# Ranking the weight splits higher and moving a scan's stores to another queue in a hybrid layer's step

## The chip, the cores and the metric

The kernel runs on one core of one Trainium2 chip. The metric is the device time of that core in microseconds (us), the median of three executions. All arithmetic is in fp32; a matmul operand in fp32r is a rounded copy of an fp32 tile.

Engines are named as the profile names them: PE (TensorE, matmuls), DVE (VectorE), ACT (ScalarE), POOL (GpSimd) and SP (SyncE). SP does nothing here but issue DMA transfers. POOL issues transfers too, and does some elementwise work. Each engine carries out its own instructions strictly in their order, and waits at the head of that order for whatever the instruction needs.

## The reference, cut to what matters

One step of a decoder layer for 256 prompt tokens and 8 sample sequences of 4 tokens (288 columns in all), with an SSD branch, a GLA branch, cross attention into 256 memory rows, and a convolutional FFN:

```python
xn = _rmsnorm(x, p['norm_mix'])
z, xbc, dt_raw, q, k, v, r, g_lr, gate_a, gate_b = _split(xn @ p['w_in'], IN_SIZES)
...
y_ssd, ssd_state_new = _ssd_scan(...)          # 4 groups, state (heads, 64, 128) per sequence
branch_a = u @ p['w_ssd_out']
...
o, gla_state_new = _gla_scan(qh, kh, vh, glog, gla_state.astype(f32))   # 4 heads, state 256x512
branch_b = o @ p['w_gla_out']
merged = jax.nn.sigmoid(gate_a) * branch_a + jax.nn.sigmoid(gate_b) * branch_b
h = x + merged @ p['w_mix_out']
h = h + _cross_attend(_rmsnorm(h, p['norm_cross']), mem_k, mem_v, p['w_cq'], p['w_co'])
up = _rmsnorm(h, p['norm_ffn']) @ p['w_up']
...
h = h + (jax.nn.silu(gt) * a) @ p['w_down']
```

The updated states of both scans are outputs: for each GLA head one 256x512 state of the prompt and eight of the samples, 512 KB each.

## The kernel before

**Products.** Activations lie transposed in SBUF, features on the partitions, 288 columns of tokens. A weight tile of 512 KB (`raw`, three buffers) is loaded in SP's queue (`wload`, L108). Each of its halves, 128x512, is split by `wsplit`: ACT copies it to a rounded `whi` (L101), DVE subtracts to get the rest, `wlo` (L103); each has five buffers (`WB`). PE then makes three products per tile, `whi` by the high part of the activations (L133), `whi` by their low part (L134) and `wlo` by the high part (L137). One split feeds 12 matmuls of 128x288. The memory projections do the same with 128x512 matmuls (L315, L316, L319).

**Stages in order of time.** Memory keys and values (to about 207 us), the four SSD groups (to 665), the four GLA heads (to 1165), gates and the mix, cross attention (1432 to 1643), the FFN, and a short tail. Within a stage `weave` (L158) runs a stream of weight products and, between its steps, steps of a background generator such as a scan, so that the PE has products to do while the scan's small operations run elsewhere.

**What sets the order.** The framework orders each engine's instructions by a priority (at first the place in the program) and its own estimate of when operands are ready. Only the first memory projection is ordered by hand (`manual_schedule`, L344 on). The state loads are put under `keep_in_program_order`.

**The start.** `mem_load` brings 256 KB of memory rows, `wload` 512 KB of weights, in turns. PE first does 9 products of ones (L349), then transposes (L287), then the first products with weights (L315).

**An SSD group's norm.** DVE adds three squares (L898), PE sums them over the partitions (L909), ACT makes the reciprocal root (L205, L206, with a table load before each), DVE scales (L914) and splits (L171).

**A GLA head's scan** (`gla_scan`, L1000 to L1140). The prompt's state `sn` is made in two chunks (L1087 is the second chunk's update) and stored (L1099). Then `load_state` (L1008) brings the sample states `sin` of sequences 0 to 3. PE adds eight products of these to `la` (L1110, each shown as a weight load and two records), four updates follow (L1119 on PE, L1120 on DVE), and after each update the state is stored (L1123) and the state four further on is loaded. The second half does the same with sequences 4 to 7. The products of a half take the last loaded state first (`for j in (3, 2, 1, 0)`). `sn` and `sin` share six buffers.

**The other stores that the change touches.** `acum_d` (L498), the convolution's last rows (L592), an SSD group's prompt state (L753) and sample states (L872), and the merged gate pieces `ma` (L1165), all in SP's queue, between the weight loads.

## Time and profile before

| | us |
|---|---|
| median of 3 executions | 2574.29 |
| lowest and highest | 2574.22, 2579.31 |
| the profiled execution | 2576.44 |
| its span | 2574.7 |
| its mean granted PE clock | 0.997 |

The span is the time between the first and the last instruction of the profiled execution; its own time is 1.7 us longer. "Idle before, releaser" in a row is how long the engine stood still before that instruction, and what it had waited for. A matmul's record lasts longer than its share of the engine, since they overlap: what counts is the distance between two starts. The granted clock is a share of full speed. A row of the view of waits gives the waiting instruction, who ended the wait, and in total, how often, and the longest. Times of DMA "to landing" run from the issue of a transfer to its arrival.

### The profile page before, as it was taken

Reading aid. Unit: us, or ns where it says so; the run is one execution under the profiler, and the core shown is the slowest. Engines: PE = TensorE matmul, PEld = TensorE weight load, DVE = VectorE, ACT = ScalarE, POOL = GpSimd, SP = SyncE. Lnnn points to the kernel's source line nnn. Section 1 sums busy time; section 2 is a strip of 40 time slices with the busy share of each in tenths; the row PEclk is TensorE's granted clock in tenths of the full one; section 3 lists DMA queues with packets and bytes.
Section 4 is the critical chain, followed back from the end, with each engine's and each line's share of the span. In section 5 each row is a group of like instructions: output and inputs, shape, how many; then the busy total and the mean of one; then the engine's idle time right before and its main releaser. Section 6 shows DMA issues by size and latency. Waiting matters only on the chain. (4 is left out here: it accounts for less than half of the span.)

```text
span 2574.7 us, 50424 instructions
## 1 busy us (share of the span) xinstructions
PE 2554.8 (99%) x19119; PEld 2458.4 (95%) x19119; DVE 1714.8 (67%) x3623; ACT 1378.2 (54%) x2751; POOL 355.5 (14%) x519
## 2 busy tenths in 40 slices
PE   9999999999999999999999999999999999999998
PEld 7889999999999999999999989999999999999998
DVE  5656767687767666767566555567777677675765
ACT  7656547665463555544455544445545455454545
POOL 3002101110000000010000222202212122130200
PEclk9999999999999999999999999999999999999999
DMA  8766666666558575777666778755555555555553
GB/s 258 221 215 202 183 188 203 187 203 200 176 181 275 182 251 176 235 227 251 186 208 211 253 257 303 223 162 165 166 174 171 168 164 175 169 168 173 170 170 127
DMA packets 435203, 513.53 MB, mean 199 GB/s; under 512 B 23216, under 2 KB 385072, under 8 KB 434896
## 3 DMA queue, kind: packets, MB, share of 16 engines
q1 hardware_dynamic: 407568, 422.34, 53.5%
q0 software_dynamic: 27360, 87.96, 10.3%
q8 instruction: 150, 2.46, 0.4%
q14 instruction: 93, 0.76, 0.1%
q10 hardware_dynamic: 32, 0.01, 0.0%
HBM read 464.74 MB, written 45.48 MB: 198 GB/s over the span
## 5 line engine op out<-in xcount | busy, mean ns | idle before, releaser
L103 DVE TENSOR_TENSOR wlo<-raw,whi 128x512 fp32r<-128x512 f32 x1464 | 991.5, 687 | 676.6 <-ACT whi L101 657.8
L101 ACT CAST whi<-raw 128x512 fp32r<-128x512 f32 x1464 | 897.2, 618 | 1000.0 <-PE acc L134 783.2
L133 PE MATMUL acc<-xn,whi 128*128 128x288 f32 (+1 forms) x1936 | 554.9, 302 | 0.0
L134 PE MATMUL acc<-xn,whi 128*128 128x288 f32 (+1 forms) x1936 | 541.5, 295 | 0.0
L137 PE MATMUL acc<-xn,wlo 128*128 128x288 f32 (+1 forms) x1936 | 412.1, 294 | 3.4 <-DVE wlo L103 3.4
L134 PE MATMUL acc<-hf,whi 128*128 128x288 f32 x1408 | 392.7, 295 | 0.0
L133 PE MATMUL acc<-hf,whi 128*128 128x288 f32 x1408 | 389.4, 292 | 0.0
L133 PEld LDWEIGHTS acc<-xn,whi 128*128 128x128 f32 (+1 forms) x1936 | 364.3, 188 | 9.3 <-issue 7.9
L134 PEld LDWEIGHTS acc<-xn,whi 128*128 128x128 f32 (+1 forms) x1936 | 364.6, 188 | 6.4 <-issue 4.1
L137 PEld LDWEIGHTS acc<-xn,wlo 128*128 128x128 f32 (+1 forms) x1936 | 311.1, 188 | 4.1 <-DVE wlo L103 4.1
L137 PE MATMUL acc<-hf,wlo 128*128 128x288 f32 x1408 | 296.2, 291 | 0.0
L134 PEld LDWEIGHTS acc<-hf,whi 128*128 128x128 f32 x1408 | 264.5, 188 | 0.1
L133 PEld LDWEIGHTS acc<-hf,whi 128*128 128x128 f32 x1408 | 264.1, 188 | 0.1
L137 PEld LDWEIGHTS acc<-hf,wlo 128*128 128x128 f32 x1408 | 225.9, 188 | 0.0
L1520 POOL COPY fsp<-fst 128x16 f32<-128x16 f32 x88 | 127.6, 1452 | 640.3 <-ACT fca L1526 286.5
L134 PE MATMUL acc<-pr,whi 128*128 128x288 f32 x704 | 196.5, 295 | 0.0
L133 PE MATMUL acc<-pr,whi 128*128 128x288 f32 x704 | 195.6, 294 | 0.0
L137 PE MATMUL acc<-pr,wlo 128*128 128x288 f32 x704 | 147.8, 291 | 0.0
L133 PE MATMUL acc<-un,whi 128*128 128x288 f32 x512 | 146.1, 301 | 0.0
L134 PE MATMUL acc<-un,whi 128*128 128x288 f32 x512 | 143.1, 295 | 0.5 <-DVE un L171 0.5
L134 PEld LDWEIGHTS acc<-pr,whi 128*128 128x128 f32 x704 | 132.3, 188 | 0.0
L133 PEld LDWEIGHTS acc<-pr,whi 128*128 128x128 f32 x704 | 132.1, 188 | 0.0
(515 smaller groups left out, 4243.1 us busy)
## 6 DMA issues: line engine op xcount, KB each, us to landing
raw<-in_w_in_dram SPq DMA_DIRECT2D x240, 512.0 KB
raw<-in_w_up_dram SPq DMA_DIRECT2D x176, 512.0 KB
raw<-in_w_down_dram SPq DMA_DIRECT2D x88, 512.0 KB
raw<-in_w_ck_dram SPq DMA_DIRECT2D x32, 512.0 KB
raw<-in_w_cv_dram SPq DMA_DIRECT2D x32, 512.0 KB
raw<-in_w_ssd_out_dram SPq DMA_DIRECT2D x32, 512.0 KB
sin<-in_state_gla_dram POOLq DMA_DIRECT2D x32, 512.0 KB, 6.2
out_dram<-sin SPq DMA_DIRECT2D x32, 512.0 KB
```

Of the source, the lines that this page charges most:

```text
L101: S.copy(hi, raw)
L103: V.tensor_tensor(lo, raw, hi, ALU.subtract)
L133: MM(a, hi[:, k, cs], xh, start=(k0 + s0 + k == 0), stop=False)
L134: MM(a, hi[:, k, cs], xl, start=False, stop=False)
L137: MM(a, lo[:, k, cs], xh, start=False, stop=(k0 + s0 + k == nk - 1))
L1520: G.tensor_copy(sp[:, :, 0:2], st.rearrange("p (b k) -> p b k", k=2))
```

## The change

- `wsplit` runs under `tc.high_priority(100)`: the splits of weights rank a hundred instructions higher in the order of ACT and DVE.
- 92 stores move from SP's queue to POOL's: the convolution's rows, the states of both scans, `acum_d` and `ma`.
- The first weight tile comes in two loads of 256 KB.
- Six products of ones stand on PE after the second transposes and before the first products with weights.
- x is loaded in every second step of the background, which has 28 steps instead of 24, and the squares of x are taken in another order. The masks' POOL operations stand later in the program.

```diff
+AHEAD = 100
...
     def wsplit(raw):
-        hi = wp.tile(list(raw.shape), F32R, tag="whi", bufs=WB, name="whi")
-        S.copy(hi, raw)
-        lo = wp.tile(list(raw.shape), F32R, tag="wlo", bufs=WB, name="wlo")
-        V.tensor_tensor(lo, raw, hi, ALU.subtract)
+        with tc.high_priority(AHEAD):
+            hi = wp.tile(list(raw.shape), F32R, tag="whi", bufs=WB, name="whi")
+            S.copy(hi, raw)
+            lo = wp.tile(list(raw.shape), F32R, tag="wlo", bufs=WB, name="wlo")
+            V.tensor_tensor(lo, raw, hi, ALU.subtract)
         return hi, lo
-    def wload(src):
+    def wload(src, apart=False):
         raw = wp.tile([P, src.shape[1], src.shape[2]], F32, tag="raw", bufs=RB, name="raw")
-        nc.sync.dma_start(out=raw, in_=src)
+        if apart:
+            for k in range(src.shape[1]):
+                nc.sync.dma_start(out=raw[:, k, :], in_=src[:, k, :])
+        else:
+            nc.sync.dma_start(out=raw, in_=src)
         return raw
...
             mem_prep(kk)
+            if kk == 1:
+                for _ in range(6):
+                    MM(wm[:, 0:P], ones, ones, start=True, stop=True)
...
         def x_norm():
...
-            xl = x_load()
-            for _ in range(4):
-                next(xl)
+            for step in range(23):
+                if step % 2 and step < 18:
+                    x_load(step // 2)
...
-        weave(chain(mem_proj(I["w_cv"], 0, o_pmv), mem_proj(I["w_ck"], 1, o_pmk)), x_norm(), 2 * KT, 24)
+        weave(chain(mem_proj(I["w_cv"], 0, o_pmv), mem_proj(I["w_ck"], 1, o_pmk)), x_norm(), 2 * KT, 28)
...
-            nc.sync.dma_start(out=acum_d, in_=acumT)
+            G.dma_start(out=acum_d, in_=acumT)
...
-                nc.sync.dma_start(out=o[:, c0:c0 + n * P].rearrange("k (t p) -> k t p", p=P), in_=st[r0:r1])
+                G.dma_start(out=o[:, c0:c0 + n * P].rearrange("k (t p) -> k t p", p=P), in_=st[r0:r1])
...
-        nc.sync.dma_start(out=o_pssd[0, h0:h0 + 8].rearrange("(t e) x n -> (e x) t n", e=2),
+        G.dma_start(out=o_pssd[0, h0:h0 + 8].rearrange("(t e) x n -> (e x) t n", e=2),
...
-                nc.sync.dma_start(out=o_sssd[2 * q + e, h0:h0 + 8].rearrange("(t e) x n -> (e x) t n", e=2),
+                G.dma_start(out=o_sssd[2 * q + e, h0:h0 + 8].rearrange("(t e) x n -> (e x) t n", e=2),
...
-        nc.sync.dma_start(out=o_pgla[0, h].rearrange("(k p) v -> p k v", p=P), in_=sprev)
+        G.dma_start(out=o_pgla[0, h].rearrange("(k p) v -> p k v", p=P), in_=sprev)
         for b in range(4):
             load_state(b)
...
-                nc.sync.dma_start(out=o_sgla[b, h].rearrange("(k p) v -> p k v", p=P), in_=sin)
+                G.dma_start(out=o_sgla[b, h].rearrange("(k p) v -> p k v", p=P), in_=sin)
                 if b + 4 < NB:
                     load_state(b + 4)
...
-            nc.sync.dma_start(out=(mg_d if t < 2 * GH else ma_d)[:, t - 3:t + 1, :], in_=ma[:, t - 3:t + 1, :])
+            G.dma_start(out=(mg_d if t < 2 * GH else ma_d)[:, t - 3:t + 1, :], in_=ma[:, t - 3:t + 1, :])
```

The changed kernel's numbers of lines differ by a few: L101 and L103 become L103 and L105, L133, L134 and L137 become L139, L140 and L143, L914 becomes L922, L1008 becomes L1016, L1099 becomes L1107, L1110 becomes L1118, L1123 becomes L1131.

POOL's order from the end of the SSD groups into the GLA heads, before (a row is a run of equal instructions, `x6` is six of them; `gw` is a gate's weights, `gq` a gate's piece):

```order
136 L699 DMA sin<-in_state_ssd_dram 128x4x128 x16
137 L947 DMA gw<-in_w_gla_gate_dram 16x256 x3
138 L1162 DMA gq<-ga_d 128x576 x4
139 L1008 DMA sin<-in_state_gla_dram 128x2x512 x6
140 L947 DMA gw<-in_w_gla_gate_dram 16x256 x3
141 L1008 DMA sin<-in_state_gla_dram 128x2x512 x8
```

The same place after, for the first GLA head:

```order
185 L1170 DMA gq<-ga_d 128x576 x4
186 L1107 DMA out_dram<-sn 128x2x512
187 L1016 DMA sin<-in_state_gla_dram 128x2x512 x4
...
192 L1131 DMA out_dram<-sin 128x2x512
193 L1016 DMA sin<-in_state_gla_dram 128x2x512
194 L1131 DMA out_dram<-sin 128x2x512
...
198 L1131 DMA out_dram<-sin 128x2x512
199 L1016 DMA sin<-in_state_gla_dram 128x2x512
200 L1131 DMA out_dram<-sin 128x2x512
201 L1016 DMA sin<-in_state_gla_dram 128x2x512
202 L1131 DMA out_dram<-sin 128x2x512 x4
```

The first four state loads now stand behind the store of `sn`, and the last of the other four behind the stores of the first four updates. The other heads read alike.

PE's order around the first products with states in that head, before:

```order
4048 L133 MATMUL acc<-un,whi 128x288
4049 L134 MATMUL acc<-un,whi 128x288
4050 L137 MATMUL acc<-un,wlo 128x288 x2
4051 L1105 MATMUL la<-vst,atsl 128x512
4052 L1110 MATMUL la<-sin,qdm 32x512 x8
4053 L133 MATMUL acc<-un,whi 128x288
```

And after:

```order
4056 L143 MATMUL acc<-un,wlo 128x288 x2
4057 L1113 MATMUL la<-vst,atsl 128x512
4058 L139 MATMUL acc<-un,whi 128x288
4059 L140 MATMUL acc<-un,whi 128x288
4060 L139 MATMUL acc<-un,whi 128x288
4061 L140 MATMUL acc<-un,whi 128x288
4062 L143 MATMUL acc<-un,wlo 128x288 x2
4063 L139 MATMUL acc<-un,whi 128x288
4064 L140 MATMUL acc<-un,whi 128x288
4065 L139 MATMUL acc<-un,whi 128x288
4066 L140 MATMUL acc<-un,whi 128x288
4067 L143 MATMUL acc<-un,wlo 128x288 x2
4068 L1118 MATMUL la<-sin,qdm 32x512 x8
```

Twelve matmuls of weights now stand between `la`'s first product and those with states; in the second and third head too, and 29 in the fourth. A head's second eight products with states stand ten matmuls later in the first three heads, and 29 in the fourth. The rest of PE's order stays, but for a few single matmuls and the six products of ones.

DVE's order around the norm of the last SSD group, before:

```order
639 L898 TENSOR_TENSOR sqa<-sqa,th 128x288
640 L990 TENSOR_TENSOR ke<-acc,ke 128x288
641 L991 TENSOR_TENSOR kd<-acc,kd 128x288
642 L992 TENSOR_TENSOR kde<-acc,kde 128x128
643 L103 TENSOR_TENSOR wlo<-raw,whi 128x512 x2
644 L914 TENSOR_TENSOR sz<-sz,rstd 128x288 x3
645 L171 SCALAR_TENSOR_TENSOR un<-sz,vcol,un 128x288 x3
```

And after (L906 is L898 before; its last row here ends the adds):

```order
713 L906 TENSOR_TENSOR sqa<-sqa,th 128x288
714 L105 TENSOR_TENSOR wlo<-raw,whi 128x512
715 L906 TENSOR_TENSOR sqa<-sqa,th 128x288
716 L105 TENSOR_TENSOR wlo<-raw,whi 128x512
717 L1000 TENSOR_TENSOR kde<-acc,kde 128x128
718 L635 COPY ksr<-kd 128x256
719 L105 TENSOR_TENSOR wlo<-raw,whi 128x512
720 L635 COPY ker<-ke 128x256
721 L922 TENSOR_TENSOR sz<-sz,rstd 128x288 x3
722 L105 TENSOR_TENSOR wlo<-raw,whi 128x512
723 L177 SCALAR_TENSOR_TENSOR un<-sz,vcol,un 128x288 x3
```

Counted from the start of the program, 424 splits stand ahead of L922 here, 420 before; ahead of the last of the three adds it is 422 and 418.

More of the change, by code (lines that the diff above doesn't have):

```diff
@@ L254, in hybrid_step @@
         mn_lo = p0.tile([P, KT, SEQ], F32R, name="mn_lo")
-        for r in range(4):
-            q = slice(r * NS, (r + 1) * NS)
-            G.affine_select(smask4[q], causal[q, q], pattern=[[-4, NB], [0, NL]], compare_op=ALU.is_ge, fill=0.0, base=0,
-                            channel_multiplier=1)
-            G.affine_select(bmask[q], ones[q, 0:NB], pattern=[[-4, NB]], compare_op=ALU.is_ge, fill=0.0, base=0,
-                            channel_multiplier=1)
-            G.affine_select(bmask[q], bmask[q], pattern=[[4, NB]], compare_op=ALU.is_ge, fill=0.0, base=3,
-                            channel_multiplier=-1)
-        V.tensor_copy(smaski, smask4)
-        gm_f = p0.tile([P, P], F32, name="gm_f")
-        G.affine_select(gm_f, causal, pattern=[[-64, 2], [0, 64]], compare_op=ALU.is_ge, fill=0.0, base=0,
-                        channel_multiplier=1)
-        V.tensor_copy(gmask, gm_f)
         vrow = p0.tile([P, P], F32, name="vrow")
@@ L299, in feed @@
                         mem_load(k0)
-                    raw = wload(w[k0 * P:(k0 + 2) * P, 512 * hd:512 * hd + 512].rearrange("(k p) n -> p k n", p=P))
+                    raw = wload(w[k0 * P:(k0 + 2) * P, 512 * hd:512 * hd + 512].rearrange("(k p) n -> p k n", p=P),
+                                prep is not None and k0 == 0)
                     for k in range(2):
@@ L371, in hybrid_step, with x_load @@
                 :, q * 512:(q + 1) * 512].rearrange("r (t p) -> t r p", p=P))
-        def x_load():
-            tc.keep_in_program_order(nc.sync.dma_start(out=xs[0:NS], in_=I["x_sample"].rearrange("b l d -> (b l) d")))
-            yield
-            for i in range(2):
-                for q in range(4):
-                    cs = slice(q * 512, (q + 1) * 512)
-                    tc.keep_in_program_order(nc.sync.dma_start(out=xp[:, i, cs], in_=I["x_prompt"][0, i * P:(i + 1) * P, cs]))
-                    yield
+        def x_load(n):
+            if n == 0:
+                d = nc.sync.dma_start(out=xs[0:NS], in_=I["x_sample"].rearrange("b l d -> (b l) d"))
+            else:
+                i, cs = (n - 1) // 4, slice((n - 1) % 4 * 512, (n - 1) % 4 * 512 + 512)
+                d = nc.sync.dma_start(out=xp[:, i, cs], in_=I["x_prompt"][0, i * P:(i + 1) * P, cs])
+            tc.keep_in_program_order(d)
         def x_norm():
@@ L385, in x_norm, with square @@
             ss = p0.tile([P, 3], F32, name="ss")
-            xl = x_load()
-            for _ in range(4):
-                next(xl)
-                yield
-            V.tensor_reduce(mrs, mss, AX.X, ALU.add)
-            S.activation(mrs, mrs, ACT.Ln, scale=1.0 / D, bias=epsc[:, 0:1])
-            S.activation(mrs, mrs, ACT.Exp, scale=-0.5)
-            next(xl)
-            yield
-            next(xl)
-            yield
-            next(xl)
-            held.pop()()
-            yield
-            for i in (2, 0, 1):
-                for q in range(4):
-                    junk = p0.tile([P, 512], F32, name="junk")
-                    S.activation(junk, xts[i][:, q * 512:(q + 1) * 512], ACT.Square, accum_out=sp4[:, i, q:q + 1])
-                    next(xl, None)
-                    yield
+            def square(i, q):
+                junk = p0.tile([P, 512], F32, name="junk")
+                S.activation(junk, xts[i][:, q * 512:(q + 1) * 512], ACT.Square, accum_out=sp4[:, i, q:q + 1])
+            for step in range(23):
+                if step % 2 and step < 18:
+                    x_load(step // 2)
+                if step == 3:
+                    V.tensor_reduce(mrs, mss, AX.X, ALU.add)
+                    S.activation(mrs, mrs, ACT.Ln, scale=1.0 / D, bias=epsc[:, 0:1])
+                    S.activation(mrs, mrs, ACT.Exp, scale=-0.5)
+                if step == 6:
+                    held.pop()()
+                if step > 6 and step % 2 == 0 and step < 15:
+                    square(2, step // 2 - 4)
+                if step > 6 and step % 2:
+                    square((step - 7) // 8, (step - 7) // 2 % 4)
+                yield
             V.tensor_reduce(ss, sp4, AX.X, ALU.add)
@@ L456, in x_prep @@
                 yield
-        weave(chain(mem_proj(I["w_cv"], 0, o_pmv), mem_proj(I["w_ck"], 1, o_pmk)), x_norm(), 2 * KT, 24)
+        for c in range(4):
+            q = slice(c * NS, (c + 1) * NS)
+            G.affine_select(smask4[q], causal[q, q], pattern=[[-4, NB], [0, NL]], compare_op=ALU.is_ge, fill=0.0, base=0,
+                            channel_multiplier=1)
+            G.affine_select(bmask[q], ones[q, 0:NB], pattern=[[-4, NB]], compare_op=ALU.is_ge, fill=0.0, base=0,
+                            channel_multiplier=1)
+            G.affine_select(bmask[q], bmask[q], pattern=[[4, NB]], compare_op=ALU.is_ge, fill=0.0, base=3,
+                            channel_multiplier=-1)
+        V.tensor_copy(smaski, smask4)
+        gm_f = p0.tile([P, P], F32, name="gm_f")
+        G.affine_select(gm_f, causal, pattern=[[-64, 2], [0, 64]], compare_op=ALU.is_ge, fill=0.0, base=0,
+                        channel_multiplier=1)
+        V.tensor_copy(gmask, gm_f)
+        weave(chain(mem_proj(I["w_cv"], 0, o_pmv), mem_proj(I["w_ck"], 1, o_pmk)), x_norm(), 2 * KT, 28)
         weave(chain(mem_proj(I["w_cv"], 1, o_pmv), mem_proj(I["w_ck"], 2, o_pmk)), x_prep(), 2 * KT - 2, 18)
```

## The prediction

> **What bounds the kernel now.** I read the page first, then the waits of the matmul engine, then the timeline around each of them.

> ```profile
> span 2574.7 us, 50424 instructions
> PE 2554.8 (99%) x19119; PEld 2458.4 (95%) x19119; DVE 1714.8 (67%) x3623; ACT 1378.2 (54%) x2751; POOL 355.5 (14%) x519
> ...
> PE acc L315 <- ACT whi L101: 3.5, 3, 1.9
> PE acc L137 <- DVE wlo L103: 3.4, 3, 2.0
> PE mm L349 <- DVE epsc L76: 1.1, 1, 1.1
> PE mm L1618 <- ACT h L1605: 0.8, 1, 0.8
> PE mm L909 <- DVE sqa L898: 0.7, 1, 0.7
> PE acc L134 <- DVE un L171: 0.5, 1, 0.5
> PE acc L133 <- ACT co L174: 0.4, 1, 0.4
> ...
> SPq L1123 <- DVE sin L1120: 39.3, 25, 3.4
> ...
> ACT whi L101 <- DMA raw<-in_w_in_dram: 55.7, 25, 5.6
> ```

> PE is busy for 2554.8 of 2574.7 us. The rows of waits (total, times, longest) sum to 10.4 us, of which 1.1 (the program's start) and 0.8 (L1618, the last stage) lie where the change does nothing. So about 8.5 us of waiting can be won, and every other engine matters only through a wait of PE. The last two rows show what this means for the stores. SP waits 39.3 us with scan stores at the head of its queue, and ACT waits 55.7 us for weights, but no such wait reaches PE: five split buffers lie between. Taking the stores off SP is worth nothing to PE beyond those rows.

> **The start.** Columns are start, duration, engine, line; for the windows: PE's busy time and records, then PEld, DVE, ACT, POOL, the granted clock, DMA share, GB/s.

> ```profile
> 1.13 3.77 PE L349 MATMUL mm<-ones 128*128 128x128 f32 x18 [1.13 <-DVE epsc L76]
> 5.01 0.44 PE L287 MATMUL mm<-ident,mt 128*128 128x128 f32 x2
> 7.62 0.74 PE L315 MATMUL acc<-whi,mn_hi 128*128 128x512 f32 x1 [1.95 <-ACT whi L101]
> 6.95 0.62 ACT L101 CAST whi<-raw 128x512 fp32r<-128x512 f32 x1 [0.98 <-DMA raw<-in_w_ck_dram]
> 8.00:9.00 1.00, 1.00 (x3) 0.72 (x3) 1.00 (x4) 0.45 (x1) 1.00 (x2) 0.50 1.07 404
> 11.00:12.00 1.00, 1.00 (x6) 0.87 (x5) 0.51 (x2) 1.00 (x3) 1.00 (x3) 0.94 0.89 159
> ```

> The memory rows are there at 5.01, the 512 KB of weights behind them at 6.95. With the weights in two halves I put the first at the middle, 5.95, so the first L315 starts 1.0 earlier. After 1.95 us of idle the clock is 0.50 to about 11.1. The six fill-in products are 12 records; 18 took 3.77, so 12 take at most 2.5 us and fit into the former idle time at the clock's full rate. If they keep the clock, 3.4 us at half rate, worth up to 1.7, go; but loads also limit this stretch. I take 1.0 each: **-2.0** (-0.8 to -2.7; the lower end is the earlier half with half of the clock's remainder lost to loads). Were the weights not early, the products alone would still leave a wait of about 1.3.

> **x every second step.** Two of the three L315 waits, 3.5 - 1.9 = 1.6 us together, are for a split whose weights stand behind x loads in SP's queue; these are now spread. **-1.6** (0 to -1.9).

> **Splits ranked higher.**

> ```profile
> 503.41 0.53 PE L137 MATMUL acc<-xn,wlo 128*128 128x288 f32 x2 [0.55 <-DVE wlo L103]
> 508.57 0.72 PE L909 MATMUL mm<-sqa,ones 128*128 128x288 f32 x2 [0.68 <-DVE sqa L898]
> 520.29 0.53 PE L137 MATMUL acc<-xn,wlo 128*128 128x288 f32 x2 [0.79 <-DVE wlo L103]
> 730.50 0.53 PE L137 MATMUL acc<-xn,wlo 128*128 128x288 f32 x2 [2.03 <-DVE wlo L103]
> 723.40 1.28 ACT L205 ACT_TABLE_LOAD   x1
> 725.00:728.00 3.00, 3.00 (x25) 3.00 (x24) 1.01 (x3) 2.96 (x6) 0.00 (x0) 1.00 0.63 175
> 731.00:734.00 3.00, 3.00 (x16) 3.00 (x15) 3.00 (x7) 0.62 (x1) 0.00 (x0) 0.56 0.57 156
> 734.00:737.00 3.00, 3.00 (x22) 3.00 (x21) 0.44 (x3) 0.81 (x2) 0.00 (x0) 0.88 0.98 288
> 722.58 0.75 PE L909 MATMUL mm<-sqa,ones 128*128 128x288 f32 x2
> 722.09 0.44 DVE L898 TENSOR_TENSOR sqa<-sqa,th 128x288 f32<-128x288 f32 x1
> ```

> The wait of 2.03 stands behind the norm chain of the last SSD group: from 723.40 ACT loads tables and DVE holds L914 for them, with too few wlo ahead. The DVE rows of the changed program put four more wlo ahead of L914, each feeding 12 matmuls, so this wait goes. So does its clock: 25 matmuls start in 3 us before it, 16 and 22 in the windows after it, 12 short at 0.12 us each, 1.4 us. -2.0 - 1.4 = **-3.4** (0 to -3.6). The waits of 0.55 and 0.79 are the same kind: **-1.3** (0 to -1.3). The price: the third L898 ends at 722.53 and L909 starts at 722.58, so there is no slack, and four wlo more stand ahead of that L898 in DVE's order, 2.6 us of DVE. I take half, since DVE has idle time further up for the rest: **+1.3** (0 to +2.6). At 508.57 one more wlo also stands ahead of L898, but other work leaves: 0 (-0.7 to +0.7). The two waits for L171 and L174 I leave, 0 (-0.9 to +1.6, the upper end the same step for other consumers of DVE). Together with the start: -2.0 - 1.6 - 3.4 - 1.3 + 1.3 = **-7.0**.

> **Stores in POOL's queue.** The other moved stores stand where POOL has nothing urgent behind them: SSD state loads run two pairs ahead, the `ma` stores wait for vector work that is done long before the states behind them are due, the conv stores and the mask's pieces are small: 0 (0 to +2). The GLA heads differ. Before, POOL issued a head's first four states 33 us before PE's use; now they stand behind the store of `sn`, and the last state behind the stores of the first four updates, and a queue's head blocks what follows.

> ```profile
> 749.79 2.91 POOL L1008 DMA_DIRECT2D sin<-in_state_gla_dram  x4 [0.99 <-issue]
> 773.68 0.74 DVE L1087 SCALAR_TENSOR_TENSOR sn<-sn,elp,mm 128x512 f32<-128x512 f32 x1
> 780.52 0.43 PE L137 MATMUL acc<-un,wlo 128*128 128x288 f32 x2
> 781.31 0.43 PE L137 MATMUL acc<-un,wlo 128*128 128x288 f32 x2
> 782.69 1.50 PE L1110 MATMUL la<-sin,qdm 128*32 128x512 f32 x12
> 930.99 0.75 DVE L1120 SCALAR_TENSOR_TENSOR sin<-sin,eb,mm 128x512 f32<-128x512 f32 x1 [0.74 <-PE mm L1119]
> 935.63 1.93 PE L1110 MATMUL la<-sin,qdm 128*32 128x512 f32 x16
> L1008 POOL DMA_DIRECT2D sin<-in_state_gla_dram x32: 707/724/765, 749.8 to 1156.3; - x32
> DMA to landing us min/median/max: 4.0/6.2/8.9
> ...
> DMA to landing us min/median/max: 5.0/6.0/7.3
> DMA to landing us min/median/max: 5.0/6.2/8.9
> DMA to landing us min/median/max: 6.0/7.6/9.6
> ```

> The landing rows, from a transfer's issue to its arrival, are of all 32 state loads, of the four at 749.79, of the four at 1123.24, and of five cache loads of the same 512 KB issued at once at 1432.36. In a burst the last one is the latest.

> *First half of a head.* `sn` is done at 774.42; PE's use was at 782.69, 8.27 us later. Six matmuls take 0.79 (780.52 to 781.31), and the order puts 12 more ahead of the use: 8.27 + 1.58 = 9.85. The store and four loads issue at 0.72 each, so the last load starts at 2.9 and lands 7.3 to 9.6 later, at 10.2 to 12.5; by the 8.9 of the burst at 1123, 11.8. The products begin with the last state, so PE waits 2.0 (0.4 to 2.7). Three heads have this gap; the fourth has its use 29 matmuls later instead of 12, which I count at 1.4 (0 to 2.1). Sum **+7.4** (1.2 to 10.2).

> *Second half.* The last L1120 of the first half ends at 931.74, the use follows at 935.63, 3.89 later; ten matmuls more (1.3) make 5.2. The store issues for 0.75, the last load lands 6.2 later (4.0 to 8.9) at 7.0. PE waits 1.8, and I take 2.0 for the store's own bytes ahead of it; **+8.0** over four heads (0 to 18).

> *Clock.* Two waits of 1.95 and 2.03 were each followed by 3.4 us at half rate, a wait of 1.34 (the next largest) was not. The grid of these 3.4 us stretches lies anyhow against the new waits; some 2 us fall inside one in about 4 of 10 cases, so 8 x 0.4 x 1.5 = **+5** (0 to +12).

> [...]

> **The sum.** -7.0 + 7.4 + 8.0 + 5 = +13.4 on the profiled execution's 2576.44. That execution lies 2.15 over the median of the runs; the difference goes onto the median 2574.29, which gives 2587.7. I round down to **2586**, since landings may gain from a SP queue without stores.

> **The rivals.**

> *A: the states land in time; slower turns to faster.* It decides at 9.85 - 2.9 = 6.9 us of landing in the first half and 5.2 - 0.75 = 4.4 in the second. For it: the burst at 749.79 had 7.3 at most, the least single landing was 4.0. Against it: 8.9 and 9.6 in the other bursts, a median of 6.2. Only the -7.0 are left: 2567. Chance 0.18.

> *B: short waits.* Landings of 7.5 in the bursts and 5.2 single give eight waits of about 0.7, too short for the clock: -7.0 + 5.6 = -1.4, 2573. Chance 0.22.

> [...] Chance 0.03. [...]

> *D: the edit doesn't do what it says*: the ranking leaves the waits of 0.55 to 2.03, and the states still wait: 13.4 + 4.7 = +18, 2592. Chance 0.07.

> My forecast has 0.50; it and C and D are slower, A is faster, B is within 0.2%, which is about what a measurement of this kernel can tell from no change (5.1 us either way). The forecast's own lower bounds (9 us of new waits and no clock) reach into that band, which gets 0.05 of its chance. So slower 0.55, same 0.27, faster 0.18. Range 2566 to 2597: A's time to D's and half of the clock's excess; below and above lie some 0.2.

> **What would show it.** Right: PE rows of L1110 (now L1118) that wait for a DMA of `sin`, up to eight, with clocks of 0.5 behind some; POOL rows where the sn store waits for DVE L1087 and four loads follow. No wait at the first L315, none for wlo near 730, one before L909 near 722. Wrong: L1110 without waits (A), POOL issues well over 0.77 us (C), or PE waits for weights in the stages where no store was moved.

## The result, and the profile after

The changed kernel takes 2610.65 us (median of 4 executions, 2609.25 to 2616.92), the kernel before 2576.6 beside it: 1.0137 of it, with a 95% interval of 1.0122 to 1.0152. It is slower by 34 to 35 us. The forecast was 2586, the range ended at 2597. The profiled execution of the changed kernel took 2616.92 and is the longest of the four; that matters below.

First the page of the changed kernel, then its matmul engine's waits (total, times, longest).

```profile
span 2615.2 us, 50509 instructions
PE 2576.7 (99%) x19131; PEld 2472.4 (95%) x19131; DVE 1719.1 (66%) x3623; ACT 1382.9 (53%) x2751; POOL 351.2 (13%) x612
```

```profile
PE la L1118 <- DMA sin<-in_state_gla_dram: 23.6, 8, 5.1
PE mm L344 <- DVE epsc L77: 1.1, 1, 1.1
PE mm L917 <- DVE sqa L906: 1.1, 1, 1.1
PE mm L1626 <- ACT h L1613: 0.8, 1, 0.8
PE acc L139 <- DVE ma L935: 0.8, 1, 0.8
PE acc L311 <- DVE wlo L105: 0.5, 1, 0.5
PE mm L278 <- DMA mt<-in_mem_prompt_dram: 0.4, 1, 0.4
PE acc L139 <- ACT co L180: 0.4, 1, 0.4
```

The waits for splits are gone but for 0.5 us, and eight waits for states have come, 23.6 us. POOL issues 400 transfers instead of 307, so 93 stores have moved, not 92. PE's busy time has grown by 21.9 us (2576.7 - 2554.8) with 12 records more, so PE also did the same work more slowly. A way to place this is to look at the start of one and the same matmul in both traces, on both sides of the GLA heads. Before:

```profile
741.09 0.38 PE L1027 MATMUL mm<-ident,vT 128*128 128x128 f32 x2
...
1170.63 0.40 PE L1119 MATMUL mm<-vst,kb 128*128 128x512 f32 x1
```

After:

```profile
734.32 0.49 PE L1035 MATMUL mm<-ident,vT 128*128 128x128 f32 x3
...
1199.49 0.55 PE L1127 MATMUL mm<-vst,kb 128*128 128x512 f32 x1
```

At the first GLA head the changed kernel is 6.8 us ahead, and 430 us later it is 28.9 us behind: 35.6 us are lost in the heads. The lag is then 33.7 at 1440 us of the kernel before, 35.6 at 2010 and 40.8 at 2461. These later steps stand beside no wait and at a granted clock of 1.00; they are taken up in the last section.

The eight waits, in the timeline of PE, with the sixteen records that follow each:

```profile
779.52 3.25 PE L1118 MATMUL la<-sin,qdm 128*32 128x512 f32 x16 [1.97 <-DMA sin<-in_state_gla_dram]
...
816.92 3.64 PE L1118 MATMUL la<-sin,qdm 128*32 128x512 f32 x16 [5.05 <-DMA sin<-in_state_gla_dram]
...
913.27 3.50 PE L1118 MATMUL la<-sin,qdm 128*32 128x512 f32 x16 [2.53 <-DMA sin<-in_state_gla_dram]
...
948.27 1.92 PE L1118 MATMUL la<-sin,qdm 128*32 128x512 f32 x16 [2.72 <-DMA sin<-in_state_gla_dram]
...
1042.08 2.99 PE L1118 MATMUL la<-sin,qdm 128*32 128x512 f32 x16 [2.18 <-DMA sin<-in_state_gla_dram]
...
1077.42 3.35 PE L1118 MATMUL la<-sin,qdm 128*32 128x512 f32 x16 [3.02 <-DMA sin<-in_state_gla_dram]
...
1166.06 1.92 PE L1118 MATMUL la<-sin,qdm 128*32 128x512 f32 x16 [1.90 <-DMA sin<-in_state_gla_dram]
...
1193.84 3.64 PE L1118 MATMUL la<-sin,qdm 128*32 128x512 f32 x16 [4.24 <-DMA sin<-in_state_gla_dram]
```

The first half of each head waits 1.97, 2.53, 2.18 and 1.90, the second 5.05, 2.72, 3.02 and 4.24. The second column tells the clock: the group takes 1.92 us at full clock, as before, and up to 3.64 at half. Two of eight kept the clock.

POOL's timeline shows the mechanism, first the start of the first head, then the last load of its second half:

```profile
767.94 0.73 POOL L1107 DMA_DIRECT2D out_dram<-sn  x1 [25.91 <-DVE sn L1095]
768.67 2.89 POOL L1016 DMA_DIRECT2D sin<-in_state_gla_dram  x4
...
805.57 0.73 POOL L1016 DMA_DIRECT2D sin<-in_state_gla_dram  x1
807.66 0.73 POOL L1131 DMA_DIRECT2D out_dram<-sin  x1 [1.35 <-DVE sin L1128]
808.38 0.73 POOL L1016 DMA_DIRECT2D sin<-in_state_gla_dram  x1
```

POOL stood 25.91 us at the store of `sn` while the four loads behind it had nothing to wait for. The landing rows of the transfers issued in these two stretches (the four loads; then the last load together with the store just ahead of it):

```profile
DMA to landing us min/median/max: 6.2/7.6/8.6
DMA to landing us min/median/max: 7.8/8.1/8.5
```

### The profile page after: what moved, and what is told of

It reads as the page before. It is cut to its first block, busy times and chain, and to the rows that moved or that the text cites. A ratio compares the mean times of both kernels' runs of the same rounds, so it can differ in the third digit from the quotient of the medians.

```text
span 2615.2 us, 50509 instructions
## 1 busy us (share of the span) xinstructions
PE 2576.7 (99%) x19131; PEld 2472.4 (95%) x19131; DVE 1719.1 (66%) x3623; ACT 1382.9 (53%) x2751; POOL 351.2 (13%) x612
## 5 line engine op out<-in xcount | busy, mean ns | idle before, releaser
L105 DVE TENSOR_TENSOR wlo<-raw,whi 128x512 fp32r<-128x512 f32 x1464 | 1004.4, 688 | 706.8 <-ACT whi L103 668.9
L103 ACT CAST whi<-raw 128x512 fp32r<-128x512 f32 x1464 | 898.8, 617 | 1006.2 <-PE acc L140 849.4
L139 PE MATMUL acc<-xn,whi 128*128 128x288 f32 (+1 forms) x1936 | 555.9, 302 | 0.0
L140 PE MATMUL acc<-xn,whi 128*128 128x288 f32 (+1 forms) x1936 | 541.4, 295 | 0.0
L143 PE MATMUL acc<-xn,wlo 128*128 128x288 f32 (+1 forms) x1936 | 412.9, 294 | 0.0
L140 PE MATMUL acc<-hf,whi 128*128 128x288 f32 x1408 | 392.8, 295 | 0.0
L139 PE MATMUL acc<-hf,whi 128*128 128x288 f32 x1408 | 391.8, 293 | 0.0
L140 PEld LDWEIGHTS acc<-xn,whi 128*128 128x128 f32 (+1 forms) x1936 | 364.2, 188 | 6.4 <-issue 4.1
L139 PEld LDWEIGHTS acc<-xn,whi 128*128 128x128 f32 (+1 forms) x1936 | 363.8, 188 | 6.8 <-issue 6.2
L143 PEld LDWEIGHTS acc<-xn,wlo 128*128 128x128 f32 (+1 forms) x1936 | 310.6, 188 | 3.9 <-issue 3.9
L143 PE MATMUL acc<-hf,wlo 128*128 128x288 f32 x1408 | 299.3, 294 | 0.0
L140 PEld LDWEIGHTS acc<-hf,whi 128*128 128x128 f32 x1408 | 264.8, 188 | 0.1
L139 PEld LDWEIGHTS acc<-hf,whi 128*128 128x128 f32 x1408 | 264.4, 188 | 0.1
L143 PEld LDWEIGHTS acc<-hf,wlo 128*128 128x128 f32 x1408 | 225.5, 188 | 0.0
L139 PE MATMUL acc<-pr,whi 128*128 128x288 f32 x704 | 196.9, 295 | 0.1
L140 PE MATMUL acc<-pr,whi 128*128 128x288 f32 x704 | 196.7, 295 | 0.0
L1528 POOL COPY fsp<-fst 128x16 f32<-128x16 f32 x88 | 53.4, 609 | 718.0 <-DVE fsp L1530 508.8
L143 PE MATMUL acc<-pr,wlo 128*128 128x288 f32 x704 | 148.9, 292 | 0.0
L139 PE MATMUL acc<-un,whi 128*128 128x288 f32 x512 | 147.1, 302 | 0.8 <-DVE ma L935 0.8
L140 PE MATMUL acc<-un,whi 128*128 128x288 f32 x512 | 143.9, 296 | 0.0
L139 PEld LDWEIGHTS acc<-pr,whi 128*128 128x128 f32 x704 | 132.2, 188 | 0.3 <-DVE h L1598 0.3
L140 PEld LDWEIGHTS acc<-pr,whi 128*128 128x128 f32 x704 | 132.4, 188 | 0.0
```

The source lines that it names most:

```text
L103: S.copy(hi, raw)
L105: V.tensor_tensor(lo, raw, hi, ALU.subtract)
L139: MM(a, hi[:, k, cs], xh, start=(k0 + s0 + k == 0), stop=False)
L140: MM(a, hi[:, k, cs], xl, start=False, stop=False)
L143: MM(a, lo[:, k, cs], xh, start=False, stop=(k0 + s0 + k == nk - 1))
L1528: G.tensor_copy(sp[:, :, 0:2], st.rearrange("p (b k) -> p b k", k=2))
```

## The experiments

Each ratio is to the kernel before, timed beside it on the same chip (its medians there 2576 to 2581).

| run | what it is | median us | ratio | interval |
|---|---|---|---|---|
| e1, again as e1b | GLA stores and `ma` on SP, rest of the change | 2583.2, 2581.4 | 1.0023, 1.0019 | 1.0013-1.0034, 1.0010-1.0029 |
| e2 | before, only `sn` and `sin` stores on POOL | 2612.4 | 1.0130 | 1.0110-1.0151 |
| e3 | `sn` and `ma` on SP, `sin` stores on POOL | 2608.5 | 1.0125 | 1.0109-1.0141 |
| e4 | loads written ahead of the stores | 2588.5 | 1.0040 | 1.0028-1.0053 |
| e5 | before, rank alone | 2580.9 | 1.0006 | 0.9995-1.0017 |
| e6 | start alone | 2579.0 | 0.9991 | 0.9978-1.0003 |
| e7, again as e7b | before, SSD stores alone on POOL | 2581.4, 2581.1 | 1.0016, 1.0019 | 1.0003-1.0029, 1.0008-1.0030 |
| e8 | rank and start, all stores on SP | 2580.2 | 0.9996 | 0.9985-1.0007 |
| e9 | changed kernel with fill-in products at the waits | 2620.7 | 1.0165 | 1.0148-1.0183 |
| e10 | e8, rank off from the first GLA head on | 2572.4 | 0.9978 | 0.9967-0.9989 |
| e11 | changed kernel, SSD stores on SP | 2618.9 | 1.0162 | 1.0149-1.0175 |

### Are the GLA stores on POOL the cause? e1 and e2

```diff
-        G.dma_start(out=o_pgla[0, h]...                 # e1: back to SP; e2: to POOL in the kernel before
+        nc.sync.dma_start(out=o_pgla[0, h]...
-                G.dma_start(out=o_sgla[b, h]...
+                nc.sync.dma_start(out=o_sgla[b, h]...
-            G.dma_start(out=(mg_d if t < 2 * GH else ma_d)...   # e1 alone
+            nc.sync.dma_start(out=(mg_d if t < 2 * GH else ma_d)...
```

> The changed kernel with the GLA stage's stores (sn, sin and the gate pieces ma) back in SP's queue; all else of the change stays. Theory (the states' loads wait behind stores in POOL's queue, and each wait brings half clock): no PE wait for a DMA of sin, clock 1.0 from the start to the tail, 7 us under the kernel before, about 2568. Rival 1 (a part of the 35 us lies in the splits' rank or the SSD stores on POOL, outside the GLA heads): over 2580. Rival 2 (the slower matmul pitch seen in some long stretches of the changed kernel's trace at full granted clock, 134 against 130 to 132 ns, comes with the change): it stays, some 5 to 10 us over 2568.

> The kernel before with only the sn and sin stores of the GLA heads moved to POOL. Theory: eight PE waits at L1110 of 20 to 27 us together, six to nine stretches of half clock, and the old waits of the kernel before kept: 36 us over it, about 2611. Rival (the splits that run further ahead are what leaves DVE's updates and POOL's stores late): the waits are under half of 23.6 us, under 2592.

The waits of PE in e1:

```profile
PE la L1118 <- DMA sin<-in_state_gla_dram: 3.0, 1, 3.0
```

And in e2:

```profile
PE la L1110 <- DMA sin<-in_state_gla_dram: 24.1, 8, 4.7
```

e2 has the whole loss, 1.0130 against 1.0137, with 24.1 us of waits and five stretches of half clock: the GLA stores on POOL are enough by themselves, and the rank is not what makes the states late. e1 takes 7 of the 8 waits away and most of the loss with it. But it came out at 2583, not at the 2568 expected, so the rest of the change does not win 7 us in the end. Its trace is 6.9 us ahead of the kernel before at 741 us and gives 5.0 of it back by 860, at the one wait that is left; most of the rest goes after 1800 us, where its matmul pitch is slow (last section). Rival 1 had something.

### Which half, and can the loads be freed? e3 and e4

e3 is the changed kernel with two of the three stores moved back, e4 leaves all the scan's stores on POOL and moves `ma` back as well:

```diff
-        G.dma_start(out=o_pgla[0, h]...                             # e3
+        nc.sync.dma_start(out=o_pgla[0, h]...
-            G.dma_start(out=(mg_d if t < 2 * GH else ma_d)...       # e3 and e4
+            nc.sync.dma_start(out=(mg_d if t < 2 * GH else ma_d)...
...
-        G.dma_start(out=o_pgla[0, h]..., in_=sprev)                 # e4
         for b in range(4):
             load_state(b)
+        G.dma_start(out=o_pgla[0, h]..., in_=sprev)
...
-                G.dma_start(out=o_sgla[b, h]..., in_=sin)
                 if b + 4 < NB:
                     load_state(b + 4)
+                G.dma_start(out=o_sgla[b, h]..., in_=sin)
```

> The changed kernel with the store of sn and the gate pieces ma back on SP, the stores of sin left on POOL: the loads of a head's first four states no longer stand behind sn. Theory: the four waits of the first halves (8.6 us in the changed kernel) and their clock go, the four of the second halves (15.0 us) and theirs stay: 2568 + 15 + 8 = 2591. Rival (the queue is full whatever its order, and the first halves wait all the same): over 2600.

> The changed kernel with ma back on SP and the scan's stores left on POOL, but each state's load written ahead of the store it stood behind: the first four loads ahead of the store of sn, the load of state b+4 ahead of the store of state b. Theory (only the place behind a waiting store costs): no PE wait for sin, 2568 as with the stores on SP. Rival (stores in the same queue slow the loads behind them, wherever they stand): second halves still wait by over 1 us each, 2575 or more.

e3's waits:

```profile
PE la L1118 <- DMA sin<-in_state_gla_dram: 15.4, 4, 4.4
PE mm L917 <- DVE sqa L1025: 5.7, 2, 3.9
```

e4's:

```profile
PE la L1118 <- DMA sin<-in_state_gla_dram: 4.4, 2, 3.6
PE mm L917 <- DVE sqa L1025: 3.1, 2, 1.6
```

In e3 the four waits of the first halves go and the four of the second stay, 15.4 us, as in the changed kernel (15.0): each half has its own cause, as the theory has it. The total did not follow (2608 against 2591): there is a new wait of 5.7 us before L917, for the squares of L1025, and there were nine half-clock stretches where the expectation had the first halves' go. In front of both of these squares DVE holds a split that waits for ACT (1.9 us at 850.92, 3.9 at 985.70). The late second halves are not shown to be behind it, since e4 has two such waits as well.

e4 shows that the place behind a waiting store is what costs: with the scan's stores in the same queue, 23.6 us of waits become 4.4, 3.6 of them in the fourth head's second half, which had no slack to begin with (in the kernel before the last state lands there at 1163.56 and is used at 1163.67). PE's order moved with the loads: in e4 the products with states stand where they stood in the kernel before (in one place one matmul later), 10 to 28 matmuls earlier than in the changed kernel, and still hardly wait. It is 1.0040, so it does not reach 2568 either: from 741 to 1200 us its trace loses 10.1 us, of which these waits, those before L917 and one half-clock stretch make 9.2.

### What the rest of the change does: e5, e6, e8, e10

e5 is the kernel before with `tc.high_priority(100)` around the splits and nothing else. e8 is the changed kernel with all its stores back on SP, e6 is that without the rank, and e10 is e8 with the rank taken off in the GLA heads:

```diff
-        with tc.high_priority(AHEAD):        # e6, around the four lines of the split
...
-            G.dma_start(out=...              # e6, e8 and e10, all seven moved lines
+            nc.sync.dma_start(out=...
...
     for n in range(8):
+        if n == 4:          # from the first GLA head on
+            rank[0] = 0     # wsplit: with tc.high_priority(rank[0])
```

> The kernel before with the splits ranked 100 instructions higher and nothing else. Theory: the waits for wlo at 503, 520 and 730 go with the clock behind the last (-5), a wait of about 1.1 comes before L909 near 722, the start is as before: 4 us under the kernel before, about 2572. Rival (the rank sets off the slow matmul pitch, 134 ns, in the FFN around 2300 to 2460, seen in the changed kernel and the three kernels that keep the rank): 5 to 8 us more, 2577 to 2580, and this stretch is in the trace.

> The changed kernel without the rank and with all stores back on SP: only the two loads, the six products of ones, x every second step and the later masks are left. Theory: 2.7 us won by 75 us, nothing after, pitch in the FFN as before: 2572 to 2573. Rival (the slow pitch comes from the start, since it shifts everything behind it): 134 ns around 2300 to 2460, 2577 to 2580.

> The changed kernel with all stores back on SP: rank and start are left. Theory (waits alone): -7 at 740 us, 2568. Rival (rank brings the slow pitch): -7 at 740, but given back between 1900 and 2460, 2575 to 2580. If neither shows the slow pitch, it is the SSD stores on POOL that set it.

> Rank and start with all stores on SP, and the rank taken off from the first GLA head on. Theory (the rank's gain of 4 us by 740 is given back at the one wait for sin of 2.5 to 3.8 us that the three kernels with the rank show near 810): no such wait, 7 us under the kernel before from 740 to the end, 0.997 of it, but for the pitch of PE, which varies from run to run by 5 us either way. Rival (the wait near 810 comes from PE being 7 us earlier, not from the rank in that head): the wait stays, ratio 0.999 to 1.000.

e5's waits show why the rank comes to nothing:

```profile
PE la L1112 <- DMA sin<-in_state_gla_dram: 2.5, 1, 2.5
...
PE mm L911 <- DVE sqa L900: 1.1, 1, 1.1
```

The waits for wlo of 0.55, 0.79 and 2.03 are gone, for one of 1.1 before L911 and one of 2.5 with a half-clock stretch in the first GLA head. (A wait of 2.0 for a wlo at 22 us is in this trace too. The kernel before has none there in its first trace and 1.1 in its second, so it is not counted against the rank.) In e8 the wait in the head is longer:

```profile
PE la L1118 <- DMA sin<-in_state_gla_dram: 3.8, 1, 3.8
```

The timeline of e8's POOL and, below it, of the kernel before shows where it comes from:

```profile
803.68 0.74 POOL L1016 DMA_DIRECT2D sin<-in_state_gla_dram  x1 [10.51 <-DMA out_dram<-sin]
```

```profile
803.15 0.74 POOL L1008 DMA_DIRECT2D sin<-in_state_gla_dram  x1 [2.68 <-DVE sin L1120]
```

The last load needs the buffer of state 1, so it waits for that state's store. In e8 SP issued this store at 793.38 and the load could follow 10.3 us later, in the kernel before at 798.42 and at most 4.7 later. So the state lands no earlier, at 810.26 against 810.20, while PE comes 7.1 us earlier to a use that had 3.4 us of slack: 3.8 us of waiting. With the rank, a store of `ma` stands ahead of the slow store and two weight loads behind it, and the load of another state, issued at 792.41, took 9.4 us as well. That these transfers hold one another up is my estimate; no run isolates it. From 49 us on, the rank alone (e5) wins 4.3 us by 741 us and gives 4.6 back near 810; e8 gives 6.7 back there.

e10 keeps the rank where it helps. The wait for a state near 810 is gone, as the theory has it, and it runs at 0.9978 (0.9967 to 0.9989): the version that beats both kernels, the one before by 0.2%. Its profiled execution is the longest of its twelve (2582.58) and shows that most of the gain can still be lost:

```profile
PE la L1120 <- DMA sin<-in_state_gla_dram: 2.9, 1, 2.9
PE acc L141 <- ACT whi L105: 1.3, 1, 1.3
```

It is 7.1 us ahead of the kernel before at 741 us. By 860 it has lost 1.8 of this, with the wait for a split at 804.70, and by 1170 another 4.5, with the wait for a state in the fourth head's second half, at 1161.25, and the half-clock stretch behind it.

The start alone (e6) is 2.2 us ahead of the first trace of the kernel before at 49 us. That is too little for its interval, and the second trace of the kernel before is 1.1 us ahead there with no change at all. The slow pitch that three expectations name as a rival, 134 ns near 2350 us, stands in e5 and not in e6 or e8; it also stands in the second trace of the kernel before, so neither the rank nor the start is needed for it.

### Is it the SSD stores? e7, e11, and e7 and e1 again

```diff
-            nc.sync.dma_start(out=acum_d, in_=acumT)      # e7, e7b: from the kernel before; e11: the other way, from the changed one
+            G.dma_start(out=acum_d, in_=acumT)
-                nc.sync.dma_start(out=o[:, c0:c0 + n * P]...
+                G.dma_start(out=o[:, c0:c0 + n * P]...
-        nc.sync.dma_start(out=o_pssd[0, h0:h0 + 8]...
+        G.dma_start(out=o_pssd[0, h0:h0 + 8]...
-                nc.sync.dma_start(out=o_sssd[2 * q + e, h0:h0 + 8]...
+                G.dma_start(out=o_sssd[2 * q + e, h0:h0 + 8]...
```

> The kernel before with only the SSD side's stores on POOL (acum_d, the convolution's rows, sf and the SSD states). Theory: no wait of PE on it, within 2 us of the kernel before. Rival: state loads of the SSD groups come late (waits at L850), over 5 us more.

> The changed kernel with only the SSD side's stores (acum_d, convolution, sf, SSD states) back on SP; the GLA stores and ma stay on POOL. Theory (the GLA queue alone): same as the changed kernel within 2 us, about 2610, eight waits for sin. Rival (the SSD stores on POOL cost 4 to 7 us by themselves): 2603 to 2606.

> Only the SSD side's stores on POOL, a second time. If they cost something, it is again 1.001 to 1.003 of the kernel before; the profile then shows either waits of PE between 200 and 740 us or the 134 ns pitch in the FFN. If it was chance, the ratio is within 0.001 of 1.

> Rank, start and the SSD side's stores on POOL, GLA stores and ma on SP, a second time. If the SSD stores cost 4 to 7 us, it is again 1.002 or more, against 0.9996 of the same kernel with all stores on SP; if it was chance, about 1.000.

The SSD stores alone on POOL cost 0.0016 and 0.0019 of the time, 4 to 5 us, twice; e1 repeats too, at 1.0023 and 1.0019. The two traces have two new waits, 1.4 at L835 in the third SSD group and 0.5 to 1.5 for a state of the fourth GLA head, which do not make 5 us; the rest of the lag in e7b's trace grows between 1500 and 2460 us without a wait. So it does in the second trace of the kernel before, so the traces do not show what the stores cost. In e11 they are back on SP and nothing is won, on the contrary: nine half-clock stretches, 2619, and longer waits for `sin`:

```profile
PE la L1118 <- DMA sin<-in_state_gla_dram: 26.2, 8, 7.4
```

So the changed kernel's 35 us are not theirs. Why they cost 4 to 5 us where they stand alone is open, and so is why e11 is slower than the changed kernel.

### The clock: e9

Eight products of ones, with an unused result, in front of each group of L1118:

```diff
         for q in range(2):
+            wf = mm_tile()
+            for _ in range(8):
+                MM(wf[:, 0:P], ones, ones, start=True, stop=True)
             for k in (1, 0):
```

> The changed kernel with eight more products of ones (about 1.8 us at full clock, their result is not used) ahead of each sixteen records of L1118; in the first three heads they stand directly ahead of it, in the fourth further up. Theory (a wait of 1.9 us or more inside one 3.4 us stretch halves the next one): the products fill PE's wait, what is left of six waits is mostly under 1.9 us, and half-clock stretches fall from 8 to 3 or 4: 5 to 8 us under the changed kernel, 2602 to 2606, although PE does 3.6 us more in the fourth head. Rival (the clock costs nothing, the waits alone count): 3.6 us over it, 2614.

The time went up by 7 to 10 us (1.0165 against 1.0137, 2620.7 against 2610.65), and the reason is in the order: the scheduler put the group with its products directly behind `la`'s first product, 12 matmuls earlier than in the changed kernel (10 in the second halves of the first three heads), so the products filled time in which PE had had work. The waits stayed (25.5 us, 1.9 more), the products cost 8 x 1.95 = 15.6 us, and the half-clock stretches fell from eight to five, worth 5.5. That sum, 12, is what the trace has lost against the changed kernel's by 1200 us (41.1 us behind the kernel before instead of 29.3). It fits half-clock stretches that stand behind idle PE, as in the last section, but the run doesn't isolate their cost, and the changed kernel's own second trace has six stretches instead of eight without any such products. The first group (the window holds the end of the wait and the group):

```profile
780.00:783.00 3.00, 2.30 (x19) 0.86 (x20) 0.00 (x0) 0.40 (x1) 0.00 (x0) 1.00 1.06 395
```

With 1.47 us of waiting left instead of 1.97 the clock stays at 1.00, where the changed kernel had 0.62 between 779 and 783. In its second trace the changed kernel waits 1.70 there and keeps the clock too.

### Both kernels once more

> The changed kernel once more, for a second profile. If the slow pitch belongs to the kernel, it stands again in the same two stretches, 1260 to 1440 and 2340 to 2500; if it is a matter of the execution, it stands elsewhere or not at all. The eight waits for sin are 20 to 27 us in both cases.

> The kernel before once more, for a second profile. If the stretches of faster and slower matmul pitch are a matter of the execution, those of 130.0 ns from 1900 to 2500 stand elsewhere or read 131.7 or 134.4; the waits of PE stay the same to 0.3 us each.

The second trace of the changed kernel, of an execution of 2610.25 us, has the same eight waits:

```profile
PE la L1118 <- DMA sin<-in_state_gla_dram: 24.3, 8, 7.1
```

In the second trace of the kernel before (2581.17 us) the waits behind the memory projections are the same to 0.3 us each, as expected, but those in them are not: L315 waits 1.9 us in all instead of 3.5, and a wait of 1.1 at L319 is new. So a gain of 1 us at the start can't be told from chance. What both say of the pitch is in the last section.

## Why the prediction was wrong

The direction and the mechanism were right, the size was not: +34 to +35 where +12 was forecast. The steps that failed are two terms of the sum, the price of the second halves (+8.0, measured 15.0) and that of the clock (+5, measured about 11.5). Term by term, against the trace:

- **Start, x and rank, -7.0.** The changed kernel is 6.8 us ahead at 741 us. The parts differ a little: 2.6 by 49 us instead of 3.6 (1.5 against the second trace of the kernel before), the wait before the last group's L909 1.1 instead of 1.3, the three waits for wlo gone as forecast. What I did not see is that the rank takes slack from the first GLA head's second half (e5, e8); in the changed kernel this would lie in the wait of 5.05, but e2, without the rank, waits 4.74 there.
- **First halves, +7.4.** Measured 8.6 (1.97 + 2.53 + 2.18 + 1.90), and 8.95 in the second trace. The last of four loads, taken as 8.9 from the burst at 1123, landed after 8.6, 9.2, 8.9 and 8.5. The fourth head came out right partly by luck: 23 matmuls more stand ahead of its use, not the 29 that I had counted, so it had 0.8 us less slack.
- **Second halves, +8.0.** Measured 15.0, and 15.3 in the second trace. This is the larger of the two misses. I priced the last load at the median landing of all 32, 6.2; here it lands 8.5, 5.8, 7.2 and 8.4 after its issue, where in the first head a store, a load and another store of 512 KB go into the queue in the 3.5 us ahead of it (804.87 to 808.38) while weights go on loading. That this crowding makes the landing long is my estimate; no run tests it by itself. Beside it, POOL starts the store 0.3 us after DVE's end, and in the second head 1.1 us pass between store and load. From the end of DVE's update to the landing 8.0 to 9.5 us pass, where 7.0 was forecast; the slack, forecast as 5.2, was 4.5 in the first head and 5.2 to 5.3 in the others. I had named landings up to 8.9 as the bound and taken the middle.
- **Clock, +5.** Measured about 11.5. I gave each wait 4 chances in 10 of lying inside one stretch. Six of eight brought half clock, and two of these for two stretches, eight of 3.41 us, 27.3 us in all; in 4.3 of them PE stood still, and the other 23.0 ran at half rate and lost half of their time. In the second trace it is six stretches and 9.3 us. I had priced a wait of the second halves at 2.0 us; those of 3.02, 4.24 and 5.05 us were each followed by half clock, that of 2.72 was not.
- **The sum.** -6.8 + 8.6 + 15.0 + 11.5 = 28.3, against the lag of 28.9 behind the heads; 0.6 us is left over. That is +29 of the +34. The remaining 5 or 6 us came after 1170 us without a wait, and belong to no step of the prediction. They depend on which traces are compared: the first trace of the changed kernel gathers 11.9 there against the first of the kernel before and 5.4 against the second, its second trace 6.3 and 0.0.
- **The range.** Its upper end, 2597, took half of the clock's excess and none of the second halves', though the text gave bounds of 12 and 18 for these. Both terms depend on the same landing times and grow together; I treated them as if they would balance.
- **Rivals.** None came true. A and B needed landings that did not occur. D is refuted by the waits for wlo that went (and its +18 kept the rank's price of 1.3, which would have gone with the rank's effect). C is refuted too, since its sign was POOL issues well over 0.77 us: POOL's 32 state loads took 0.712 to 0.742 us each. The issue of these loads was never slow, POOL stood at the head of its queue.
- **"Taking the stores off SP is worth nothing."** The waits of ACT for weights fell from 55.7 to 16.3 us, and no wait of PE goes with them.

## What to carry to other kernels

Ahead of moving a transfer to another queue, write down what stands behind it there and what it waits for: a store that waits for a result, ahead of prefetches that wait for nothing, turns the prefetches into loads on demand (POOL stood 150.4 us at the four stores of `sn` alone). Price such loads by the slowest landing in a burst with the same neighbours, not by the median (here the last loads took 5.8 to 9.2 us, against a median of 6.2 before). And count a wait of PE twice: by its length, and by the half clock behind it. Here six of eight waits of 1.90 to 5.05 us, 23.6 us in all, were followed by it, and it cost about 11.5 us more.

## What the runs showed of the hardware

```profile
817.00:820.00 3.00, 3.00 (x16) 0.52 (x16) 0.00 (x0) 0.00 (x0) 0.00 (x0) 0.50 0.14 50
...
948.00:951.00 3.00, 2.73 (x22) 1.25 (x23) 0.23 (x1) 0.59 (x1) 0.00 (x0) 1.00 0.15 52
```

**The matmul pitch had three values at a granted clock of 1.00.** Windows of 50 us full of the same matmuls hold 387, 382 or 374 records (one more or less), with 130, 132 or 134 ns from start to start. The changed kernel's first trace has 134 ns from 2347 to 2501 us and 130 just ahead of it and behind it; where it changes, a few matmuls of L1547 stand between. The kernel before in its two traces, the first quoted from the first:

```profile
2350.00:2400.00 50.00, 50.00 (x387) 50.00 (x386) 35.18 (x82) 25.24 (x54) 8.34 (x6) 1.00 0.53 159
```

```profile
2350.00:2400.00 50.00, 50.00 (x375) 50.00 (x374) 33.57 (x80) 24.42 (x54) 6.62 (x5) 1.00 0.52 163
```

The changed kernel in its first and second trace:

```profile
2350.00:2400.00 50.00, 50.00 (x374) 50.00 (x373) 27.25 (x47) 19.21 (x31) 2.79 (x6) 1.00 0.55 170
```

```profile
2350.00:2400.00 50.00, 50.00 (x387) 50.00 (x386) 27.56 (x46) 19.96 (x33) 1.17 (x3) 1.00 0.54 171
```

The same program has the slow value in one execution and the fast one in another, so it belongs to the execution: 150 us at 134 instead of 130 ns cost 5 us, a good part of the spread of the times of one kernel (2573 to 2585 for the kernel before) and about what its two traces differ by (2576.44 and 2581.17). The lag that the changed kernel gathers after 1170 us, 11.9 us in the first trace and some 6 in the second, stands in such stretches. At 2350 us the slow value stands in eight of the seventeen traces: the second of the kernel before, the first of the changed kernel, and those of e1, e3, e4, e5, e10 and e11. What sets it was not settled, nor whether a part of the change makes it more frequent. The two traces of the SSD stores alone (e7, e7b) do not have it at 1300, 2100 or 2350 us, so it is not shown to be their 4 to 5 us.
